# Which flag tile each top-k selection writes: two shared tiles, or tiles by selection

## The chip, the cores and the metric

The kernel runs on one core of a Trainium2 chip. The metric is the time of one execution in microseconds (us) on the device. The engines are named as in the profile: PE (TensorE, matrix products), DVE (VectorE), ACT (ScalarE), POOL (GpSimd) and SP (SyncE, which issues DMAs). Each engine works through its own list of instructions in order.

## The reference

It is one inference step of a two-layer decoder for 1024 prompt tokens and 32 sampled tokens (8 sequences of 4). Layer 0 mixes tokens by a gated MLP. Layer 1 is a sparse attention: an indexer scores every earlier token, the 256 best are kept for each query, and only these are attended to.

```python
def dsa_prompt(h, w_in, w_out):
    q, k, v, qi, ki, wi = dsa_project(h, w_in, pos)
    k_top = min(TOPK_MAX, T // 4)                      # 256
    ...
        sc = index_scores(qi_b, wi_b, ki)
        sc = jnp.where(pos[None, None, :] <= tq[None, :, None], sc, -jnp.inf)
        _, idx = lax.top_k(sc, k_top)
        valid = idx <= tq[None, :, None]
        return attend(q_b, k[bi, idx], v[bi, idx], valid)
```

The sampled tokens do the same against a paged cache of 1024 older tokens. After the mixer of each layer comes an MLP of width 4096 with a squared relu, and a norm ends the whole.

## The kernel before

The two layers follow each other. This study is about the attention of layer 1, roughly from 1100 to 1720 us of the profiled execution. It has these parts, in the order of the code: the index scores (lines 847 to 903), the projection of the queries (lines 932 to 937, one addition of a DVE step at line 914 per result), keys (`key_tile`, KT at line 207/1010) and values, the attention of the samples against the gathered cache (`sample_keys`, `sample_softmax`, `fetch_values`, `sample_values`), and the attention of the prompt: `scores(j, kv)` for query block j (128 queries) and `values(j, kv)`.

The kernel does not gather the 256 best keys. It finds, for each query, the 256th largest index score, and turns the score row into a bias (0 for a kept key, a huge negative number for a dropped one) that `scores` adds at line 1116. Blocks 0 and 1 have at most 256 keys and need no selection. Blocks 2 to 7 have their index scores in SC[2] to SC[7] (128 x 384 up to 128 x 1024); in lists of the order these tiles carry the numbers 11964 to 11969. The samples' scores are SCS, a part of the tile ssum.

`topk` does four selections; the text calls them by their tags:

- a: the samples, one row of 1028 keys, rounds on ACT;
- b: blocks 2 and 3, rounds on DVE;
- c: blocks 4 and 5, rounds on ACT;
- d: blocks 6 and 7, rounds on DVE.

A selection first counts how many scores are at least 0 and then fixes the threshold bit by bit, in 31 rounds. A round on DVE is one count per block (line 705: compare, add up, and write the flags, which nobody reads, to a flag tile) and two small steps (lines 719 and 720). A round on ACT is one Sign per block (line 726, which writes a flag tile too) and three small DVE steps (lines 728 to 730); a selection on ACT ends with one more count per block on DVE at line 705. Then lines 737 to 746 turn the scores into the bias ("marking"). The small tiles of a selection are called sma to smd in the profile.

All counts on DVE write `junk_v` and all Signs on ACT write `junk_a`. The order on each engine is not the order of the code: the framework schedules the instructions along a simulated time line, and keeps only the orders that the tiles ask for. Two writes to one tile stay in the order of the code, also where both are on one engine and nobody reads what they wrote.

Of the kernel before, what the change touches and what calls it, by code (L numbers as in the profile page):

```python
# [14 lines left out]
I8 = mybir.dt.int8  # L15
AF = mybir.ActivationFunctionType
# [5 lines left out]
P = 128  # L22
# [17 lines left out]
L_S = PAST + 4  # L40
# [9 lines left out]
def toks(i):  # L50
    return (i * P, min(T, (i + 1) * P))
# [82 lines left out]
def build(nc, tc, I, O):  # L134
    ctx = ExitStack()
    V, S, G, PE, SP = nc.vector, nc.scalar, nc.gpsimd, nc.tensor, nc.sync

    def pool(name, stack=ctx, **k):
        return stack.enter_context(tc.tile_pool(name=name, bufs=k.pop("bufs", 1), **k))
# [14 lines left out]
    def f(ap):  # L154
        return ap.bitcast(F32)
# [196 lines left out]
    for i0, i1 in ((0, 1), (1, 3), (3, 6), (6, 9)):  # L352
# [3 lines left out]
        for k0 in range(0, NK, g):  # L356
            p = ps("px" if k0 // g % 2 else "pt")
            for k in range(k0, k0 + g):
                for i in range(i0, i1):
                    a, b = toks(i)  # L360
                    o = (k - k0) * w + a - t0
                    PE.transpose(p[:, o:o + b - a], natural(i)[:b - a, k * P:(k + 1) * P], eye[:b - a, :b - a])
            x = al.tile([P, 512], F32, name="xc", bufs=6)
# [13 lines left out]
    for qt in range(4):  # L377
# [22 lines left out]
        for i in range(NT):  # L400
            a, b = toks(i)
# [278 lines left out]
    tkp = pool("tkp", st)  # L680

    def t2(shape, d=F32R, tag="t2"):
        return tkp.tile(shape, d, name=tag, bufs=2 if tag == "tk" else 3)

    junks = [tkp.tile([P, L_S], I8, name="junk%d" % z) for z in range(2)]

    def topk(tag, blocks, how, R):
        nb = len(blocks)
        bank = tkp.tile([P, 7 * nb], F32, name="sm" + tag)
        used = [0]  # L690

        def small(name, d=F32):
            used[0] += nb
            return bank[:, used[0] - nb:used[0]].bitcast(d)

        cnt, s, lim = small("cnt"), small("s"), small("lim")
        cand, nxt, kb = small("cand", I32), small("nxt", I32), small("kb", I32)
        junk_v, junk_a = junks
        eq = small("eq")
        for z in (cnt, eq):  # L700
            G.memset(z, 0.0)

        def count(sc):
            for i, x in enumerate(blocks):
                V.tensor_scalar(junk_v[R, :x.shape[1]], x, sc if isinstance(sc, float) else sc[R, i:i + 1], None,  # L705
                                op0=ALU.is_ge, op1=ALU.add, accum_out=cnt[R, i:i + 1])

        if how == "act":
            for i, x in enumerate(blocks):
                G.memset(lim[:, i:i + 1], x.shape[1] - 2 * TOPK + 0.5)  # L710
        count(0.0)
        V.tensor_scalar(s, cnt, TOPK - 0.5, 2.0, op0=ALU.is_ge, op1=ALU.mult)
        V.tensor_scalar(s, s, 1.0, None, op0=ALU.subtract)
        V.tensor_scalar(cand, cnt, TOPK - 0.5, -1.0, op0=ALU.is_lt, op1=ALU.mult)
        V.tensor_scalar(cand, cand, 1 << 30, None, op0=ALU.bitwise_xor)
        if how == "vec":
            for bit in range(30, -1, -1):
                count(f(cand))
                V.tensor_scalar(kb, cnt, TOPK - 0.5, float(1 << bit), op0=ALU.is_lt, op1=ALU.mult)
                V.scalar_tensor_tensor(cand, kb, 1 << (bit - 1) if bit else 0, cand, op0=ALU.bitwise_xor,  # L720
                                       op1=ALU.bitwise_xor)
        else:
            for bit in range(30, -1, -1):
                for i, x in enumerate(blocks):
                    L = x.shape[1]
                    S.activation(junk_a[R, :L], x, AF.Sign, bias=f(cand)[R, i:i + 1], scale=-1.0,
                                 accum_out=cnt[R, i:i + 1])
                V.tensor_scalar(nxt, cand, 1 << (bit - 1) if bit else 0, None, op0=ALU.bitwise_xor)  # L728
                V.tensor_tensor(kb, cnt, lim, op=ALU.is_gt)
                V.scalar_tensor_tensor(cand, kb, bit, nxt, op0=ALU.logical_shift_left, op1=ALU.bitwise_xor)  # L730
            V.tensor_copy(kb, s)
            V.tensor_tensor(nxt, cand, kb, op=ALU.add)
            count(f(nxt))
            V.scalar_tensor_tensor(kb, cnt, TOPK - 0.5, s, op0=ALU.is_ge, op1=ALU.mult)
            V.tensor_tensor(cand, cand, kb, op=ALU.add)
        need = lim
        V.tensor_scalar(s, f(cand), -1.0, None, op0=ALU.mult)
        for i, x in enumerate(blocks):
            sg, e = (t2([P, L_S], d, "tk")[R, :x.shape[1]] for d in (BF16, F16))
            S.activation(sg, x, AF.Sign, bias=s[R, i:i + 1], accum_out=cnt[R, i:i + 1])  # L740
            V.tensor_scalar(e, sg, 0.0, None, op0=ALU.is_equal, op1=ALU.add, accum_out=eq[R, i:i + 1])
            V.tensor_tensor(need[:, i:i + 1], eq[:, i:i + 1], cnt[:, i:i + 1], op=ALU.subtract)
            V.tensor_scalar(need[:, i:i + 1], need[:, i:i + 1], 0.5, TOPK + 0.25 - x.shape[1] / 2, op0=ALU.mult, op1=ALU.add)
            V.tensor_tensor_scan(e, e, e, 0.0, ALU.add, ALU.max)
            V.scalar_tensor_tensor(x, e, need[R, i:i + 1], sg, op0=ALU.is_gt, op1=ALU.is_le)
            G.tensor_scalar(x, x, -DROP, DROP, op0=ALU.mult, op1=ALU.add)
# [16 lines left out]
    def select(where):  # L763
        for z, (blks, how, w) in enumerate(TOPK_GROUPS):
            if w == where:
                topk("abcdef"[z], [SCS if j == "S" else SC[j] for j in blks], how, SB if "S" in blks else slice(0, P))
# [80 lines left out]
    for i in (8, 0, 1, 2, 3, 4, 5, 6, 7):  # L847
        a, b = toks(i)
# [384 lines left out]
def trace(inputs):  # L1233
    import concourse.bacc as bacc

    nc = bacc.Bacc("TRN2", target_bir_lowering=False, num_devices=1)
    arrays, I, O = {}, {}, {}
    data = {n: np.ascontiguousarray(inputs[n]) for n in INS}
    data["one"], data["one_a"], data["ropeq"] = ONE, ONE_A, ROPEQ
    for n, a in data.items():  # L1240
        arrays["in_" + n] = a
        I[n] = nc.dram_tensor("in_" + n, a.shape, mybir.dt.from_np(a.dtype), kind="ExternalInput").ap()
    for n, s in OUTS:
        O[n] = nc.dram_tensor("out_" + n, s, F32, kind="ExternalOutput").ap()
    with tile.TileContext(nc, schedule_with_timeline_sim=True) as tc:
        build(nc, tc, I, O)
    return nc, arrays
# [8 lines left out]
```

## Time and profile before

| | us |
|---|---|
| median of 3 runs (2542.66 to 2546.99) | 2546.78 |
| the profiled execution | 2550.52 |
| its span, first to last instruction | 2548.4 |

Against the span, PE is busy for 92%, DVE for 67%, POOL for 51%, ACT for 42%. The granted TensorE clock is 0.969 of full speed in the mean. The shares are means over a long kernel, in most of which PE never stops; what counts for this change is the stretch from 1138 to 1720 us.

### The profile page before, as it was taken

How to read it: one execution, taken by the hardware profiler on the slowest of the kernel's cores; microseconds unless marked ns; L12 is line 12 of the kernel's file. 1: busy time of each engine (PE TensorE's matmuls, PEld its weight loads, DVE VectorE, ACT ScalarE, POOL GpSimd, SP SyncE). 2: the span in 40 equal slices, each digit the busy share in tenths (PEclk: the TensorE clock that was granted, in tenths of full speed). 3: DMA queues.
4: the chain of work that ended last, by engine and by line, in shares of the span. 5: the costliest groups of instructions: out<-in, count | busy, mean ns of one | idle time of the engine just before them, and what ended most of it. 6: DMA issues, size and time to landing. Idle time of an engine off the chain costs nothing.

```text
span 2548.4 us, 42829 instructions
## 1 busy us (share of the span) xinstructions
PE 2356.4 (92%) x16001; PEld 2250.2 (88%) x16001; DVE 1712.3 (67%) x3730; ACT 1063.9 (42%) x2161; POOL 1310.0 (51%) x1695
## 2 busy tenths in 40 slices
PE   8999999999999999999888786199999999999998
PEld 8999999999999999878876565089999999999998
DVE  6241277777777777836873289963777777777775
ACT  5223243333333333548426874152433333333335
POOL 2246347667666676422333342032466566666764
PEclk9999999999999999999989798599999999999999
DMA  6111301111111111322233510004111111111111
GB/s 230 50 44 50 110 30 46 51 42 51 46 47 50 47 46 51 107 61 78 67 95 116 192 26 9 0 22 143 32 46 53 42 44 53 47 50 42 51 51 69
DMA packets 180800, 158.46 MB, mean 62 GB/s; under 512 B 10376, under 2 KB 169712, under 8 KB 179568
## 3 DMA queue, kind: packets, MB, share of 16 engines
q1 hardware_dynamic: 176496, 136.86, 17.4%
q0 software_dynamic: 4096, 18.88, 2.2%
q8 instruction: 125, 2.05, 0.3%
q14 instruction: 83, 0.68, 0.1%
HBM read 134.24 MB, written 21.47 MB: 61 GB/s over the span
## 4 chain that ended last, share of the span: by engine, by line
PE 31%; DVE 10%; POOL 5%; issue 5%; DMA 3%; ACT 3%; SPq 0%; DVEq 0%; POOLq 0%; ACTq 0%
PE ps L245 4%; PE ps L250 3%; PE ps L251 3%; DVE junk L705 3%; PE px L245 3%; PE px L251 3%; PE px L250 3%; PE ps L593 1%; PE ps L594 1%; PE ps L595 1%; POOL st L561 1%; DMA qd<-scr 1%; DMA raw<-in_cache_k,idh 1%; PE pt L595 1%; PE pt L594 1%
## 5 line engine op out<-in xcount | busy, mean ns | idle before, releaser
L584 POOL TENSOR_TENSOR X<-X,scr 128x264 f32<-128x264 f32 x480 | 427.7, 915 | 166.3 <-DVE X L584 119.5
L245 PE MATMUL ps<-h,w 128*128 128x384 f32 (+1 forms) x1344 | 436.9, 325 | 3.5 <-DVE sma L728 3.0
L251 PE MATMUL ps<-h,w 128*128 128x384 f32 (+1 forms) x1344 | 434.2, 323 | 1.6 <-POOL w L207 1.4
L250 PE MATMUL ps<-h,w 128*128 128x384 f32 (+1 forms) x1344 | 434.7, 323 | 0.0
L206 ACT ACTIVATE w<-raw 128x1024 fp32r<-128x1024 f32 (+2 forms) x248 | 250.8, 1013 | 315.2 <-PE px L250 122.8
L207 DVE TENSOR_TENSOR w<-raw,w 128x1024 fp32r<-128x1024 f32 (+1 forms) x211 | 296.6, 1406 | 36.5 <-ACT w L206 36.1
L245 PE MATMUL px<-h,w 128*128 128x384 f32 (+1 forms) x960 | 311.9, 325 | 0.3
L250 PE MATMUL px<-h,w 128*128 128x384 f32 (+1 forms) x960 | 309.3, 322 | 0.0
L251 PE MATMUL px<-h,w 128*128 128x384 f32 (+1 forms) x960 | 308.7, 322 | 0.0
L606 ACT ACTIVATE scr<-ps 128x264 f32<-128x264 f32 x240 | 92.7, 386 | 425.5 <-PE ps L595 375.7
L245 PEld LDWEIGHTS ps<-h,w 128*128 128x128 f32 x1344 | 253.4, 189 | 5.2 <-DVE sma L728 3.3
L251 PEld LDWEIGHTS ps<-h,w 128*128 128x128 f32 x1344 | 253.3, 188 | 3.1 <-POOL w L207 1.7
L250 PEld LDWEIGHTS ps<-h,w 128*128 128x128 f32 x1344 | 253.3, 188 | 0.7
L584 DVE TENSOR_TENSOR X<-X,ps 128x264 f32<-128x264 f32 x480 | 197.5, 422 | 63.6 <-PE ps L595 63.6
L584 DVE TENSOR_TENSOR X<-X,px 128x264 f32<-128x264 f32 x480 | 194.4, 422 | 53.4 <-PE px L595 53.4
L593 PE MATMUL ps<-A,w 128*128 128x264 f32 x720 | 206.9, 288 | 20.8 <-ACT A L206 20.8
L584 DVE TENSOR_TENSOR X<-X,pt 128x264 f32<-128x264 f32 x480 | 203.3, 424 | 33.8 <-PE pt L595 28.8
L594 PE MATMUL ps<-A,w 128*128 128x264 f32 x720 | 206.4, 290 | 7.2 <-DVE A L207 7.0
L595 PE MATMUL ps<-A,w 128*128 128x264 f32 x720 | 203.4, 284 | 0.0
L571 POOL TENSOR_TENSOR raw<-raw 128x128 f32<-128x128 f32 x120 | 56.9, 474 | 268.9 <-DMA raw<-in_ffn_w 178.6
L207 DVE TENSOR_TENSOR A<-st,A 128x264 fp32r<-128x264 f32 (+2 forms) x184 | 163.8, 902 | 45.9 <-ACT A L206 45.9
L245 PEld LDWEIGHTS px<-h,w 128*128 128x128 f32 x960 | 180.3, 188 | 1.8 <-DVE X L584 1.7
(396 smaller groups left out, 6353.5 us busy)
## 6 DMA issues: line engine op xcount, KB each, us to landing
raw<-in_ffn_w SPq DMA_DIRECT2D x68, 512.0 KB
raw<-in_ffn_w SPq DMA_DIRECT2D x120, 256.0 KB
X<-xd SPq DMA_DIRECT2D x16, 528.0 KB
raw<-in_a_w_in SPq DMA_DIRECT2D x10, 512.0 KB
GV<-in_x_prompt SPq DMA_DIRECT2D x8, 512.0 KB
raw<-in_a_w_out SPq DMA_DIRECT2D x8, 512.0 KB
raw<-in_b_w_in SPq DMA_DIRECT2D x8, 512.0 KB
raw<-in_b_w_out SPq DMA_DIRECT2D x8, 512.0 KB
```

The lines of the kernel that those rows point to most:

```text
L206: S.activation(hi, src, AF.Copy)
L207: (lo_w[0] or V).tensor_tensor(lo, src, f(hi), op=ALU.subtract)
L245: PE.matmul(out, lh, rh, start=first, stop=False)
L250: PE.matmul(out, lh, rl, start=False, stop=False)
L251: PE.matmul(out, ll, rh, start=False, stop=last)
L571: G.tensor_tensor(sm[0], a21, a22, op=ALU.add)
L584: eng.tensor_tensor(x, x, src, op=op)
L593: PE.matmul(p, wh, xh, start=first, stop=False, skip_group_check=not first)
L594: PE.matmul(p, wh, xl, start=False, stop=False, skip_group_check=not first)
L595: PE.matmul(p, wl, xh, start=False, stop=True, skip_group_check=not first)
L606: S.activation(u, p, AF.Copy)
L705: V.tensor_scalar(junk_v[R, :x.shape[1]], x, sc if isinstance(sc, float) else sc[R, i:i + 1], None, op0=ALU.is_ge, op1=ALU.add, accum_out= ...
```

## The change

The two shared flag tiles go. Selections a, b and c each get a flag tile of their own, used by both their engines; selection d writes the tile of a (the tag is the letter; the condition is true for d alone).

```diff
-    junks = [tkp.tile([P, L_S], I8, name="junk%d" % z) for z in range(2)]
+    junks = {}
...
-        junk_v, junk_a = junks
+        if how == "vec" and tag != "b":
+            junk = junks["a"]
+        else:
+            junk = junks[tag] = tkp.tile([P, max(x.shape[1] for x in blocks)], I8, name="junk" + tag)
...
-                V.tensor_scalar(junk_v[R, :x.shape[1]], x, sc if isinstance(sc, float) else sc[R, i:i + 1], None,
+                V.tensor_scalar(junk[R, :x.shape[1]], x, sc if isinstance(sc, float) else sc[R, i:i + 1], None,
                                 op0=ALU.is_ge, op1=ALU.add, accum_out=cnt[R, i:i + 1])
...
-                    S.activation(junk_a[R, :L], x, AF.Sign, bias=f(cand)[R, i:i + 1], scale=-1.0,
+                    S.activation(junk[R, :L], x, AF.Sign, bias=f(cand)[R, i:i + 1], scale=-1.0,
                                  accum_out=cnt[R, i:i + 1])
```

No instruction is added or removed: each engine has as many as before. The tiles take 1028, 512 and 768 bytes of each partition where they took twice 1028. What changes is the order that the scheduler makes. In the changed kernel's lists the line numbers behind line 697 are higher by 3 (705 is 708).

First place, DVE: the first count of b. Before it stands here, behind the last count of a (the third row is a's last count, the last row b's first, on SC[2]):

```order
L900 SCALAR_TENSOR_TENSOR sc_11967<-r,wsc,sc_11967 128x384
L732 ISA sma<-sma 128x2
L705 TENSOR_SCALAR junk_11973,sma<-ssum,sma 32x1028
L900 SCALAR_TENSOR_TENSOR sc_11967<-r,wsc,sc_11967 128x384
L914 TENSOR_TENSOR scr<-ps,rbc 128x384
L734 SCALAR_TENSOR_TENSOR sma<-sma 128x1
L705 TENSOR_SCALAR junk_11973,smb<-sc_11964 128x384
```

Now, on DVE, in the middle of the index scores of block 4 (tile 11966), rounds of b (smb) and rounds of a (sma) stand in turns:

```order
L708 TENSOR_SCALAR junkb,smb<-sc_11964,smb 128x384
L732 TENSOR_TENSOR sma<-sma 128x1
L708 TENSOR_SCALAR junkb,smb<-sc_11965,smb 128x512
L733 SCALAR_TENSOR_TENSOR sma<-sma 128x1
L917 TENSOR_TENSOR scr<-ps,rbc 128x384
L903 SCALAR_TENSOR_TENSOR sc_11966<-r,wsc,sc_11966 128x320
L722 TENSOR_SCALAR smb<-smb 128x2
L731 TENSOR_SCALAR sma<-sma 128x1
L903 SCALAR_TENSOR_TENSOR sc_11966<-r,wsc,sc_11966 128x320
L723 SCALAR_TENSOR_TENSOR smb<-smb 128x2
```

So b has moved from behind all of a, where block 5 was being scored, to its scores' own readiness.

Second place, DVE: the end of the rounds of d, and the first step of the prompt's attention that stands behind it. Before, it is the first step of `scores(6)` (L1116 on tile 11968, block 6):

```order
L705 TENSOR_SCALAR junk_11973,smd<-sc_11969,smd 128x1024
L719 TENSOR_SCALAR smd<-smd 128x2
L720 SCALAR_TENSOR_TENSOR smd<-smd 128x2
L737 TENSOR_SCALAR smd<-smd 128x2
L741 TENSOR_SCALAR tk,smd<-tk 128x896
L742 TENSOR_TENSOR smd<-smd 128x1
L744 SCALAR_TENSOR_TENSOR tk<-tk 128x896
L743 TENSOR_SCALAR smd<-smd 128x1
L745 SCALAR_TENSOR_TENSOR sc_11968<-tk,smd 128x896
L1116 ISA w,mx<-px,sc_11968 128x448
```

Now, on DVE, the rounds of d end inside the second `sample_softmax` (L1044), and what stands behind them is the first step of `scores(0)` (L1119 on the causal mask, in the tile one):

```order
L1044 ISA mxs 128x1
L723 SCALAR_TENSOR_TENSOR smd<-smd 128x2
L1044 ISA w,mxs<-ps,w,mxs 128x260
L1044 ISA mxs 128x1
L740 TENSOR_SCALAR smd<-smd 128x2
L955 RECIPROCAL rc<-sd 128x1
L744 TENSOR_SCALAR tk,smd<-tk 128x896
L1056 TENSOR_TENSOR pn<-w,one 128x32
L745 TENSOR_TENSOR smd<-smd 128x1
L747 SCALAR_TENSOR_TENSOR tk<-tk 128x896
L746 TENSOR_SCALAR smd<-smd 128x1
L1119 ISA w,mx<-px,one 128x128
```

The whole of d has moved ahead of the whole of the prompt's attention. Third place, DVE, right behind the last index score of block 7: where before only rounds of b stood, rounds of d, c and b now share the engine:

```order
L708 TENSOR_SCALAR junka,smd<-sc_11968,smd 128x896
L731 TENSOR_SCALAR smc<-smc 128x2
L708 TENSOR_SCALAR junkb,smb<-sc_11964,smb 128x384
L917 TENSOR_TENSOR scr<-ps,rbc 128x384
L708 TENSOR_SCALAR junka,smd<-sc_11969,smd 128x1024
L708 TENSOR_SCALAR junkb,smb<-sc_11965,smb 128x512
L732 TENSOR_TENSOR smc<-smc 128x2
L722 TENSOR_SCALAR smd<-smd 128x2
L722 TENSOR_SCALAR smb<-smb 128x2
L733 SCALAR_TENSOR_TENSOR smc<-smc 128x2
```

Counted over the whole order of DVE, so many rounds of the 31 stand ahead of three steps that both kernels have:

| rounds ahead of | before: a, b, c, d | now: a, b, c, d |
|---|---|---|
| the mask of block 7 (L902), the end of the index scores | 31, 11, 0, 0 | 31, 25, 10, 0 |
| the index copy of `fetch_values` (L1064) | 31, 31, 11, 0 | 31, 31, 30, 22 |
| the first step of `scores(0)` (L1116) | 31, 31, 23, 0 | 31, 31, 31, 31 |

## Rows read from the trace of the kernel before

**Rows 1.** The page: busy tenths of PE, granted TensorE clock, 40 slices.

```profile
PE   8999999999999999999888786199999999999998
PEclk9999999999999999999989798599999999999999
```

**Rows 2.** Windows: start:end, length, busy us by engine, PEclk, DMA share, GB/s.

```profile
1138.00:1293.00 155.00, 141.75 (x847) 134.51 (x846) 119.81 (x314) 102.73 (x186) 39.63 (x38) 0.98 0.22 65
1293.00:1415.00 122.00, 101.43 (x699) 83.76 (x698) 55.80 (x195) 61.69 (x141) 48.47 (x92) 0.89 0.37 115
1415.00:1455.00 40.00, 25.15 (x146) 18.15 (x145) 8.73 (x41) 31.96 (x70) 13.76 (x15) 0.77 0.65 243
1455.00:1577.00 122.00, 105.52 (x643) 78.22 (x641) 108.46 (x345) 85.85 (x209) 47.22 (x62) 0.95 0.11 28
1577.00:1647.00 70.00, 0.00 (x0) 0.00 (x1) 64.62 (x141) 2.64 (x5) 0.94 (x1) 0.52 0.00 0
1647.00:1720.00 73.00, 70.07 (x355) 56.35 (x356) 48.29 (x118) 39.41 (x69) 22.78 (x20) 0.95 0.06 18
```

**Rows 3.** Waits of PE, 1475 to 1720: us in total, times, longest.

```profile
PE px L245 <- DVE mx L1116: 75.1, 4, 70.4
```

**Rows 4.** Timeline of PE: start, us, operation, [idle before <- releaser].

```profile
1647.00 0.74 PE L245 MATMUL px<-KT,t 128*128 128x448 f32 x1 [70.37 <-DVE mx L1116]
```

**Rows 5.** Timeline of DVE: score blocks ready (L902), counts (L705).

```profile
1173.27 0.29 DVE L902 TENSOR_TENSOR sc<-sc,one 128x128 f32<-128x128 f32 x1
...
1225.57 1.27 DVE L705 TENSOR_SCALAR_CACHE_REDUCE junk<-ssum,sma 32x1028 int8<-32x1028 f32 x1
...
1227.95 0.55 DVE L705 TENSOR_SCALAR_CACHE_REDUCE junk<-sc 128x384 int8<-128x384 f32 x1
...
1230.72 0.28 DVE L902 TENSOR_TENSOR sc<-sc,one 128x128 f32<-128x128 f32 x1
...
1292.47 0.28 DVE L902 TENSOR_TENSOR sc<-sc,one 128x128 f32<-128x128 f32 x1
...
1349.61 0.81 DVE L705 TENSOR_SCALAR_CACHE_REDUCE junk<-sc 128x640 int8<-128x640 f32 x1
...
1501.02 1.07 DVE L705 TENSOR_SCALAR_CACHE_REDUCE junk<-sc 128x896 int8<-128x896 f32 x1
```

**Rows 6.** Timeline of DVE: starts of two rounds of b, two of d.

```profile
1299.89 0.60 DVE L705 TENSOR_SCALAR_CACHE_REDUCE junk<-sc,smb 128x384 int8<-128x384 f32 x1
...
1301.73 0.61 DVE L705 TENSOR_SCALAR_CACHE_REDUCE junk<-sc,smb 128x384 int8<-128x384 f32 x1
...
1578.30 1.15 DVE L705 TENSOR_SCALAR_CACHE_REDUCE junk<-sc,smd 128x896 int8<-128x896 f32 x1
...
1581.21 1.15 DVE L705 TENSOR_SCALAR_CACHE_REDUCE junk<-sc,smd 128x896 int8<-128x896 f32 x1
```

**Rows 7.** Groups by shape, DVE, 1138 to 1650: busy, mean ns | idle before, releasers.

```profile
L914 DVE TENSOR_TENSOR scr<-ps,rbc 128x384 f32<-128x384 f32 x16 | 8.9, 555 | 10.2 <-DMA qd<-scr 3.7 <-POOL scr L928 3.6 <-PE ps L251 2.9
L729 DVE TENSOR_TENSOR smc<-smc 128x2 int32<-128x2 f32 x31 | 7.5, 243 | 53.2 <-ACT junk L726 53.2
L728 DVE TENSOR_SCALAR smc<-smc 128x2 int32<-128x2 int32 x31 | 6.4, 206 | 1.0
L729 DVE TENSOR_TENSOR sma<-sma 128x1 int32<-128x1 f32 x31 | 6.1, 196 | 15.3 <-ACT junk L726 15.1
L730 DVE SCALAR_TENSOR_TENSOR smc<-smc 128x2 int32<-128x2 int32 x31 | 5.6, 180 | 1.0
L207 DVE TENSOR_TENSOR KT<-pt,KT 128x256 fp32r<-128x256 f32 x8 | 3.4, 422 | 10.3 <-ACT KT L206 10.3
```

**Rows 8.** One line's instructions (L719): ns min/median/max, first and last start.

```profile
L719 DVE TENSOR_SCALAR smb<-smb x31: 154/169/1387, 1237.4 to 1349.5; 128x2 int32<-128x2 f32 x31
L719 DVE TENSOR_SCALAR smd<-smd x31: 149/169/509, 1513.2 to 1639.0; 128x2 int32<-128x2 f32 x31
```

**Rows 9.** The Signs of c on ACT, by tile.

```profile
L726 ACT ACTIVATE junk<-sc,smc x62: 812/888/978, 1354.0 to 1496.3; 128x640 int8<-128x640 f32 x31, 128x768 int8<-128x768 f32 x31
```

## The prediction

> **What bounds the kernel now.** I begin with the page's slices: PE is at nine tenths nearly everywhere, except around the slices from 1300 us on, with a hole of two slices in which the clock falls too [rows 1]. So I cut the attention of layer 1 into six stretches with the windows [rows 2]. In the stretch from 1577 to 1647 PE does nothing at all, while DVE is busy for 64.6 of 70 us. The waits of PE say for what: 75.1 us in four waits for DVE's step at L1116, one of 70.4 us [rows 3]; the timeline shows that one ending at 1647.00 with the first product of `scores(6)` in a new bank [rows 4]. L1116 adds the bias of block 6, and that is made by selection d, whose rounds run until 1639 [rows 8].
>
> Why is d so late? The timeline of DVE has each block's readiness and each selection's first count [rows 5]. SC[3] is ready at 1173.5, b starts at 1227.95, right behind the last count of a (1225.57). SC[5] is ready at 1231.0, c starts at 1349.6, when b's rounds are over. SC[7] is ready at 1292.8, d starts its first count at 1501.0, when c's are. The scores are ready 54, 118 and 208 us before they are used. No data goes from one selection to the next; what they share is the flag tile of the counts. The four therefore run one behind the other, and the last leaves DVE as the only working engine.
>
> **What the change removes.** With tiles of their own, b and c may start when their scores are there; d shares only with a, which ends early. The order shows that this happens: ahead of the first step of `scores(0)` stand all 31 rounds of d, where none stood. So the wait of 70.4 us [rows 4] has nothing left to wait for. I take 70, the length of the stretch, and count the restart in the last term.
>
> **What it costs.** The same rounds now stand on DVE ahead of the prompt's attention, and an engine works in order: the steps of index scores, queries, keys and `scores(0)` queue behind them. I sum DVE's work in the three stretches before 1455, where `scores(0)` starts, from its busy time [rows 2] and the rounds that the order moves. A round of b costs 1301.73 - 1299.89 = 1.84 us, one of d 1581.21 - 1578.30 = 2.91 [rows 6], the three small steps of a round of c 0.243 + 0.206 + 0.180 = 0.63 [rows 7].
> First stretch (to the end of the index scores): 119.8, plus 14 rounds of b 25.8, plus 10 of c 6.3, plus three first counts of c and d (0.8 to 1.1 each, [rows 5]) 2.9: 154.8 us of 155.
> Second (to `fetch_values`): 55.8, less 14 rounds of b 25.8, plus 9 of c 5.7, plus 22 of d 64.0, less c's first counts 1.8, plus one of d 1.2: 99.1 of 122.
> Third (to `scores(0)`): 8.7, less 11 rounds of c 6.9, plus 9 of d 26.2, plus about 9 (my estimate, from the blocks' widths) for the last counts and the marking of c: 37 of 40.
> Together 291 us of work where 317 pass. It fits, if DVE never waits; it does wait. Of its idle time, 10.2 us before L914 and 10.3 before KT come from DMAs, POOL, PE and ACT, which the change does not touch; the 15.3 for a's Signs stay in part, as b's rounds now fill them; the 53.2 for c's Signs [rows 7] shrink, since a count of d of 1.2 us now stands where DVE idled, against about 1.8 us of two Signs [rows 9]. I let 15 us remain in the first stretch, which is full, some 27 in the second, which has 23 of room, and 6 in the third, which has 3. The overrun is 15 + 4 + 3 = 22 us. Bounds: nothing, if the rounds fill every gap; and 107 (35 + 43 + 29, all that is added), if not one of them falls into idle time. I take the low part, since DVE in the stretch from 1455 to 1577, where rounds and other work stand mixed already, is busy for 108.5 of 122 us, 89% [rows 2], and 291 at 89% are 327, ten more than pass.
>
> **VectorE and GpSimd.** The rounds of d move from a stretch in which POOL works 0.94 of 70 us into one with 48.5 of 122 [rows 2]. The small step L719 shows what may come of it: the median is 169 ns for b and for d, the longest is 1387 for b, which ran beside a busy POOL, and 509 for d [rows 8]. If every third round of d's 31 lost 1.2 us so, that would be 12 us; I leave it inside the 22 and the range. The Trainium skill (SBUF — State Buffer, Who interferes with whom) states that VectorE and GpSimd share a port pair as an exclusive lock, taken by VectorE instructions with two SBUF inputs or in a two-port mode, but not by the form of tensor_scalar that writes its accumulator. By that rule only the small steps can be blocked, never the counts, which fits these rows; were all 31 rounds blocked once for the longest excess, the sum would be 37 us worse and the time 2522.
>
> **What else follows.** From 1455 to 1720 the prompt's attention took 265 us, 70 of them the stall. In the other 195 PE is busy for 105.5 + 70.1 = 175.6 and idle for 19.4, at a clock of 0.95 [rows 2]. The rounds of c and d leave this stretch, which frees over 40 us of DVE, and without the stall there is no restart at the lower clock (0.52 in the stall is near the lower of the two levels, 1.2 GHz). Full clock would give back 5% of 175.6, 9 us, and half the idle time another 10. I take 14; bounds 5 and 28. The Signs of c cost ACT the same, earlier: its stretches have 155 - 103 and 122 - 62 us free [rows 2], and c brings 10 rounds into the first. I cost that at nothing; if ACT were late, DVE's small steps of c would wait, which is in the overrun. SP's and POOL's orders change at a few places, for nothing by my count, since their waits end with data.
>
> **The sum** against the profiled execution: 2550.5 - 70 - 14 + 22 = 2488.5. That execution is 3.7 us above the median, so the forecast is 2546.8 - 62 = 2485. A change within 0.2% (5 us) is about what a measurement here can't tell from none.
>
> **Rivals.** (1) The waits of DVE are longer than I say: the chains of a, b, c and d wait for one another in one queue, each small step of c for ACT, with everything behind it. Half of the 107 us unhidden is 53; with 10 from the attention the gain is 27, the time 2520. For it speaks that 53.2 us were idled for c alone [rows 7]; against it, that the third stretch has nothing else to do than these rounds. (2) Slower: the first stretch is full by my sum, and there the index scores feed PE through ACT; if the added rounds hide nowhere, 107 - 70 - 14 gives +23, 2570. It decides from an overrun of 84 us on, almost four times mine. (3) The change does not do what it says, because another wait ends at the same place, the marking on POOL or c's 62 Signs: about 2547. Against it, the order has c and d finished before `scores(0)`, 100 us of PE work ahead of their first use. (4) Better: the gaps take all the rounds and the attention gives 28: 2449.
>
> **How the numbers follow.** My forecast, 2463 to 2514 by the bounds of the overrun (0 to 45), 0.58. Better than that 0.15. A gain of 5 to 33 us, rival 1, 0.16. No change 0.04, slower 0.07. From these faster is 0.89, same 0.04, slower 0.07. The range 2450 to 2525 leaves out the two slow cases, part of rival 1 and the last of rival 4.
>
> **What would show it.** Right: no wait of PE of over 10 us at L1116; rounds of b from about 1180, c from 1240, d from 1310; DVE over 85% busy from 1138 to about 1475; `scores(0)` 10 to 35 us later than 1455; from there to the end of the attention about 180 us. The terms are wrong if the index scores end after 1320 (the first overrun is larger), or if DVE idles for c's Signs as long as before. The prediction fails if PE waits for L1116 as long as before at `scores(0)` instead of `scores(6)`: then the stall has only moved to the front.

## The result and the profile after

The changed kernel takes 2450.26 us (median of 4 runs, 2447.63 to 2453.22), the kernel before in the same series 2546.23. The ratio is 0.9626, 95% interval 0.9609 to 0.9643: 96 us or 3.7% faster. The forecast was 2485, 62 us faster; the result lies 0.3 us inside the lower edge of the range, and the same kernel measured again (e11) took 2447.1 us, outside it. That the first number fell inside is luck. The direction and the mechanism were right, the size was short by 34 us.

The profiled execution has a span of 2451.1 us (before 2548.4). Its page, busy tenths of PE and granted clock in 40 slices, as in [rows 1]:

```profile
PE   8999999999999999989987879999999999999998
PEclk9999999999999999999999879999999999999999
```

The hole of two slices is gone, and with it the dip of the clock. The waits of PE from the start of the prompt's attention (1463.7 us) to its end (us in total, times, longest), which answer to [rows 3]:

```profile
PE ps L245 <- ACT w L206: 1.1, 1, 1.1
PE px L251 <- POOL t L207: 0.4, 1, 0.4
```

No wait for DVE's step that adds the bias (now L1119) is left. Where the rounds went is seen by tile, for b, c and d (start of the first and the last):

```profile
L708 DVE TENSOR_SCALAR_CACHE_REDUCE junkb<-sc,smb x62: 597/672/746, 1179.2 to 1323.7; 128x384 int8<-128x384 f32 x31, 128x512 int8<-128x512 f32 x31
...
L729 ACT ACTIVATE junkc<-sc,smc x62: 811/875/958, 1235.0 to 1418.7; 128x640 int8<-128x640 f32 x31, 128x768 int8<-128x768 f32 x31
...
L708 DVE TENSOR_SCALAR_CACHE_REDUCE junka<-sc,smd x62: 1133/1204/1282, 1300.3 to 1455.0; 128x896 int8<-128x896 f32 x31, 128x1024 int8<-128x1024 f32 x31
```

The rounds of b begin at 1179, where even its first count came at 1228 [rows 5]; the first Sign of c comes 119 us earlier than in [rows 9]; the rounds of d begin at 1300, where its first count came at 1501. The three overlap, and the last small step of d starts at 1457.5, ahead of the attention's start at 1463.7.

To see where the 97.3 us of the span come from, I take four steps of DVE that every kernel here has: the first use of the mask (block 0, the start of the prompt's attention), of c's bias (block 4, 128x320), of d's bias (block 6, 128x448) and the last one. First the timeline of DVE before, then after:

```profile
1455.59 0.28 DVE L1116 CUSTOM_DVE_ANT_0 w<-px,one 128x128 f32<-128x128 f32 x1
...
1513.87 0.47 DVE L1116 CUSTOM_DVE_ANT_0 w<-px,sc 128x320 f32<-128x320 f32 x1
...
1646.31 0.62 DVE L1116 CUSTOM_DVE_ANT_0 w<-px,sc 128x448 f32<-128x448 f32 x1 [1.06 <-POOL sc L746]
...
1691.79 0.74 DVE L1116 CUSTOM_DVE_ANT_0 w<-px,sc,mx 128x512 f32<-128x512 f32 x1
```

```profile
1463.73 0.28 DVE L1119 CUSTOM_DVE_ANT_0 w<-px,one 128x128 f32<-128x128 f32 x1
...
1504.84 0.48 DVE L1119 CUSTOM_DVE_ANT_0 w<-px,sc 128x320 f32<-128x320 f32 x1
...
1549.04 0.61 DVE L1119 CUSTOM_DVE_ANT_0 w<-px,sc 128x448 f32<-128x448 f32 x1
...
1595.16 0.74 DVE L1119 CUSTOM_DVE_ANT_0 w<-px,sc,mx 128x512 f32<-128x512 f32 x1
```

From these I form three intervals: A from block 0 to block 4, B from block 4 to block 6, C from block 6 to the last step. The table has them for the experiments too (us; each worked out from such rows of that kernel's profiled execution). The medians come from several series, in which the kernel before took 2546.2 to 2549.6 us; the ratios compare within a series. The marks are steps of DVE, so an interval does not hold the same PE work in every kernel: PE's products recorded in A, B without the stall, and C are 353, 288 and 198 before, 322, 268 and 254 after. The sum of the three is what can be compared most safely.

| kernel | median | ratio to before | start | A | B | C |
|---|---|---|---|---|---|---|
| before | 2546.2 | 1 | 1455.6 | 58.3 | 132.4 | 45.5 |
| changed | 2450.3 | 0.9626 | 1463.7 | 41.1 | 44.2 | 46.1 |
| changed, again (e11) | 2447.1 | 0.9610 | 1455.4 | 41.3 | 44.2 | 46.1 |
| e1 c writes a's tile, d its own | 2447.4 | 0.9608 | 1456.8 | 43.4 | 44.2 | 46.1 |
| e2 d writes c's tile | 2483.8 | 0.9746 | 1459.6 | 48.1 | 75.7 | 45.3 |
| e3 before, d with 9 rounds | 2485.5 | 0.9751 | 1457.5 | 58.3 | 68.1 | 46.5 |
| e4 only d has its own | 2491.6 | 0.9780 | 1449.4 | 92.1 | 46.1 | 46.0 |
| e5 changed, d with 8 rounds | 2450.7 | 0.9608 | 1461.0 | 42.5 | 44.2 | 46.1 |
| e6 changed, b counts twice | 2465.6 | 0.9677 | 1456.5 | 53.5 | 51.5 | 46.1 |
| e7 only c has its own | 2455.9 | 0.9635 | 1442.8 | 46.4 | 52.2 | 50.7 |
| e8 changed, scores(0) ahead of the softmax | 2456.3 | 0.9637 | 1455.8 | 55.5 | 44.7 | 46.1 |
| e9 before, d with 1 round | 2466.9 | 0.9685 | 1452.4 | 58.5 | 48.7 | 46.0 |
| e10 = e1, again | 2447.2 | 0.9602 | 1457.8 | 42.9 | 44.2 | 46.1 |
| e12 two tiles, a+c and b+d | 2452.5 | 0.9629 | 1458.4 | 46.4 | 44.3 | 46.3 |

In the profiled execution the start is 8.1 us later, A is 17.2 shorter and B 88.2, of which 70.4 are the stall of [rows 4] and 17.8 the rest; C is about the same (0.6 longer). 70.4 + 17.2 + 17.8 - 8.1 = 97.3. The windows of the changed kernel (columns as in [rows 2]) up to the start, up to the first use of d's bias, and the end of the attention:

```profile
1138.00:1463.70 325.70, 274.51 (x1715) 243.25 (x1715) 269.88 (x797) 212.87 (x435) 102.06 (x149) 0.91 0.33 106
1463.70:1549.00 85.30, 84.78 (x588) 68.63 (x578) 68.98 (x234) 65.54 (x164) 48.49 (x62) 0.99 0.13 32
1549.00:1623.00 74.00, 72.89 (x407) 61.42 (x406) 49.62 (x125) 44.66 (x79) 20.91 (x19) 1.00 0.08 23
```

In the attention PE is idle for 0.5 + 1.1 = 1.6 us, where it was idle for 19.4 beside the stall [rows 2], and its 995 products are busy for 157.7 us instead of 175.6. So both halves of the extra gain are there: 18 us of idle time and 18 of PE's busy time. The second is not all shorter products: nine products of the samples' softmax (L1050 and L1056), whose durations make 3.8 us, lie just inside the window before (from 1455) and just ahead of it now.

### The profile page after: what moved, and what is told of

It is laid out like the page before. It is cut to its first block, busy times and chain, and to the rows that moved or that the text cites. A ratio compares the mean times of both kernels' runs of the same rounds, so it can differ in the third digit from the quotient of the medians.

```text
span 2451.1 us, 42867 instructions
## 1 busy us (share of the span) xinstructions
PE 2341.6 (96%) x16001; PEld 2250.3 (92%) x16001; DVE 1689.3 (69%) x3730; ACT 1062.5 (43%) x2161; POOL 1314.2 (54%) x1695
## 4 chain that ended last, share of the span: by engine, by line
PE 36%; DVE 7%; POOL 4%; DMA 3%; issue 3%; ACT 2%; SPq 0%; DVEq 0%; POOLq 0%; ACTq 0%
PE ps L245 4%; PE ps L251 4%; PE ps L250 4%; PE px L245 3%; PE px L251 3%; PE px L250 3%; PE ps L593 2%; PE ps L594 1%; PE ps L595 1%; POOL st L561 1%; DVE sc L903 1%; PE pt L1132 1%; PE pt L595 1%; PE pt L594 1%; PE pt L593 1%
## 5 line engine op out<-in xcount | busy, mean ns | idle before, releaser
L584 POOL TENSOR_TENSOR X<-X,scr 128x264 f32<-128x264 f32 x480 | 434.7, 930 | 168.2 <-DVE X L584 119.6
L207 DVE TENSOR_TENSOR w<-raw,w 128x1024 fp32r<-128x1024 f32 (+1 forms) x211 | 292.4, 1386 | 37.7 <-ACT w L206 37.3
L571 POOL TENSOR_TENSOR raw<-raw 128x128 f32<-128x128 f32 x120 | 55.5, 462 | 262.3 <-DMA raw<-in_ffn_w 172.5
L207 DVE TENSOR_TENSOR A<-st,A 128x264 fp32r<-128x264 f32 (+2 forms) x184 | 163.5, 901 | 44.9 <-ACT A L206 44.8
```

Source lines behind the costliest of these rows:

```text
L207: (lo_w[0] or V).tensor_tensor(lo, src, f(hi), op=ALU.subtract)
L571: G.tensor_tensor(sm[0], a21, a22, op=ALU.add)
L584: eng.tensor_tensor(x, x, src, op=op)
```

## The experiments

Theory A, as the result left it: a shared flag tile costs only where the earlier selection still works when the scores of the later one are ready; the gain is the stall, plus A and B, in which rounds of c and d no longer stand among the steps of the attention; and the rounds that now stand ahead of the attention lie in idle time of DVE. The rivals: the sharing with a matters; the 35 us belong to the stall, as restart and piled-up work; a fixed share of the moved rounds is not hidden.

### Which sharing costs

**e1**, from the changed kernel. c and d swap places in the memory:

```diff
-        if how == "vec" and tag != "b":
+        if tag == "c":
             junk = junks["a"]
```

> The tiles dealt out another way: c writes the tile of a, and d has its own. Theory A (a shared tile costs only where the earlier selection is still at work when the scores of the later one are ready): a ends at 1257 us and c could start at 1231, so c starts some 25 us later than in the changed kernel, still long before its bias is wanted at about 1500: 2450 us, within 5. Rival (any sharing with a puts work into the full stretch before the queries' projection, or d was held by a): 2460 and more for the first, under 2443 for the second.

Measured: 2447.43 us, 0.9608 (0.9592 to 0.9624). The first Sign of c is at 1259 instead of 1235, as expected, and B and C are those of the changed kernel. Since this is at the edge of what a measurement can tell, the two kernels ran once more together:

> The first experiment's kernel beside the changed one on one chip. Theory A (which selection shares with a doesn't matter): a ratio to the kernel before that lies within 0.2% of the changed kernel's. Rival (d held by a's tile, or room in the first stretch since c starts later): 0.2% to 0.4% faster than the changed kernel.

> The changed kernel once more, as a yardstick for the run before it: 0.9626 of the kernel before, within 0.002.

Measured: 0.9602 (0.9589 to 0.9615) for e10 and 0.9610 (0.9596 to 0.9623) for e11, 2447.2 and 2447.1 us. They are the same within the intervals: whether c or d shares with a, which ends at 1257, makes no difference that these runs can tell.

**e2**, from the changed kernel. Now d shares with one that is not done in time (the tile of c is made 1024 wide):

```diff
-        if how == "vec" and tag != "b":
-            junk = junks["a"]
+        if tag == "d":
+            junk = junks["c"]
```

> d writes the tile of c in place of that of a, b has its own. Theory A: d can't start before c's last count at about 1425 us, so 20 of its 31 rounds stand among the steps of the prompt's attention, where DVE has some 16 of 86 us free; the attention is slower by 30 to 55 us than in the changed kernel, without one long stall: 2490 us (2480 to 2505). Rival 1 (only the one long stall counted, and rounds among the attention are hidden): 2455. Rival 2 (d is late again and PE stalls for it as before): 2530.

Measured: 2483.84 us, 0.9746 (0.9730 to 0.9763). The rounds of d, by tile, and then the longest group of PE's waits from 1440 to 1620:

```profile
L708 DVE TENSOR_SCALAR_CACHE_REDUCE junkc<-sc,smd x62: 1129/1201/1280, 1410.3 to 1574.7; 128x896 int8<-128x896 f32 x31, 128x1024 int8<-128x1024 f32 x31
```

```profile
PE px L245 <- DVE mx L1119: 14.2, 5, 10.7
```

So d starts 110 us later than in the changed kernel, though only the tile differs, and 34 of the 96 us are lost again (31 by the ratios). The wait of 10.7 us, which ends with d's bias at 1584, explains a third of it; the rest lies in A (48.1 us instead of 41.1) and in B, 75.7 us long with that wait instead of 44.2, where DVE is busy for 72.8 us. Theory A holds, rival 1 (2455) and rival 2 (2530) fall.

**e4**, from the kernel before: only d leaves the row (one tile is shared by a, b and c on both engines).

```diff
-        junk_v, junk_a = junks
+        junk_v = junk_a = junks[0] if tag != "d" else tkp.tile([P, 1024], I8, name="junk" + tag)
```

> One tile for a, b and c, and one for d: only d leaves the row of selections, and c is behind b as before and now beside d. Theory A: d's stall of 70 us goes, but 21 of c's rounds stand behind the start of the prompt's attention (in the kernel before 8), so the attention waits for c's bias at block 4 instead: about 2505 us (2485 to 2525). Rival (the long stall was all that cost): 2450 to 2476.

Measured: 2491.57 us, 0.9780 (0.9762 to 0.9797); theory A gave 2505 (2485 to 2525). B falls to 46.1, but A grows to 92.1, and the timeline of PE names the place:

```profile
1542.02 0.63 PE L245 MATMUL px<-KT,t 128*128 128x320 f32 x1 [27.08 <-DVE mx L1116]
```

That wait ends with the first step on c's bias (block 4, 320 columns, at 1541). The stall has moved from d to c. To free the last in the row is not enough.

**e7**, the same with c in place of d (`tag != "c"`):

> One tile for a, b and d, and one for c: only c leaves the row, d follows b directly. By the order 18 of d's rounds stand ahead of the attention and 13 among it, all of c ahead of it. Theory A: c's bias is early, so block 4 doesn't wait, d ends some 40 us behind its place in the changed kernel and its 13 rounds slow the first blocks by what DVE has not idle: 2470 us (2460 to 2482), the time from the start of the attention to the first use of d's bias 100 to 112 us (85 in the changed kernel, 124 with d behind c). Rival (a stall for d remains, as in the kernel before): 2500 and more.

Measured: 2455.9 us, 0.9635 (0.9620 to 0.9649). This was a miss, and neither theory had it: A and B together are 98.6 us, a little under what was expected (100 to 112), but the attention starts at 1442.8, 13 us earlier than in the kernel before. Ahead of the start PE did as much as in the others (window to that point, columns as in [rows 2]):

```profile
1138.00:1442.80 304.80, 268.10 (x1694) 235.12 (x1696) 243.05 (x708) 212.29 (x435) 108.30 (x146) 0.94 0.35 113
```

PE is idle there for 36.7 us, in the changed kernel for 51.2. One of the waits that shrink is PE's longest wait for the gather of the samples' keys, 2.3 us here, 9.2 in the changed kernel. That is half of the 14.5 us. Why this order of the rounds suits that stretch is not settled: each of these edits moves the order of every engine, not only that of the rounds. The early start is given back in the attention, where 13 rounds of d stand: A, B and C are 17.9 us longer than in the changed kernel.

**e12**, from the changed kernel: as many tiles as before, two of 1028 bytes, but dealt out by selection instead of by engine.

```diff
-        if how == "vec" and tag != "b":
-            junk = junks["a"]
+        if tag in "cd":
+            junk = junks["ab"["cd".index(tag)]]
```

> Two tiles of 1028 bytes, as many as in the kernel before, but dealt out by selection and not by engine: a and c share one, b and d the other. By the order 20 rounds of d stand ahead of the value fetch and all 31 ahead of the prompt's attention, as in the changed kernel. Theory A (it counts only whether the earlier sharer is done in time, not how many tiles there are): a is done some 25 us, b some 30 us after c's and d's scores are ready, which the attention doesn't notice: 0.960 to 0.963 of the kernel before, about 2450 us. Rival (the later start of d pushes its end into the attention, as where d followed b and c was free): 0.964 to 0.970.

Measured: 2452.54 us, 0.9629 (0.9616 to 0.9642). The ratio is that of the first measurement of the changed kernel and 0.2% above the second, so all but a few us of the gain are there, with no byte more than before. The rounds of d, by tile:

```profile
L708 DVE TENSOR_SCALAR_CACHE_REDUCE junkb<-sc,smd x62: 1131/1208/1281, 1313.5 to 1453.5; 128x896 int8<-128x896 f32 x31, 128x1024 int8<-128x1024 f32 x31
```

d waits for b here, and starts 13 us later than in the changed kernel. The attention hardly notices: B and C are the same, A is 5 us longer (46.4), with 1.8 us of waits of PE for L1119 and a granted clock of 0.89 in A, where it was 0.98. Four tiles, one for each selection, were not tried.

### What the 35 us beyond the stall are

**e3** and **e9**, from the kernel before: its order, with fewer rounds of d (9 and 1).

```diff
-            for bit in range(30, -1, -1):
+            for bit in range(30, 21 if tag == "d" else -1, -1):
                 count(f(cand))
```

> The kernel before, with 9 of d's 31 rounds; 22 rounds are left out, so the bias of blocks 6 and 7 is not the reference's. Order and tiles are as before. It takes 22 x 2.91 = 64 us out of the stall and moves nothing else. Theory A (the changed kernel's 35 us beyond the stall came from rounds of c and d that no longer stand among the attention of blocks 0 to 5): they are still there, so only the 64 go: 2483 us (2478 to 2488). Rival (the 35 us belonged to the stall itself, as restart at a low clock and work that piled up behind it): 2450 to 2460.

> The kernel before with one of d's 31 rounds; 30 are left out, so the bias of blocks 6 and 7 is not the reference's. The order of the rest is that of before. With 9 rounds it took 2485.5 us and no long stall was left, only 8 rounds among the steps of blocks 4 and 5. Theory A (rounds among the attention's steps delay PE): the 8 rounds are 23 us of DVE's work in a stretch where DVE is busy for 66 of 69 us, so most of it comes back: 2466 us (2458 to 2472), and the time from the first use of c's bias to the first of d's falls from 68 us to 45 to 52. Rival (the attention of blocks 4 and 5 is held by c's lateness and by PE's own work, the rounds of d beside it are free): 2480 to 2486.

Measured: 2485.54 us, 0.9751 (0.9732 to 0.9769) for e3, and 2466.92, 0.9685 (0.9670 to 0.9700) for e9. With 9 rounds the long stall is gone (PE waits for L1116 for 9.7 us in four pieces), but B is still 68.1 us long and the time 35 us above the changed kernel. With one round B falls by another 19.4, and as A and C stay within 0.6 us, so does the whole attention. That is 2.4 us for each of the 8 rounds (2.1 by the ratios), against 2.91 of DVE's work [rows 6]. PE's waits for the steps on d's bias (448 columns), 6.3 us of the 9.7 in e3, are gone in e9. Another wait that falls is that of PE's values products for the addition of DVE at L207, which stands in the same queue as the rounds, in e3 and then in e9 (us in total, times, longest):

```profile
PE ps L248 <- DVE raw L207: 9.9, 12, 2.0
```

```profile
PE ps L248 <- DVE raw L207: 5.0, 6, 1.4
```

In the kernel before it was 8.1 us in ten waits; in the changed kernel none is left. So of the 17.8 us of B at least 13 are rounds of d among the steps of blocks 4 and 5 (62.0 without the stall, 48.7 in e9), not a consequence of the stall. Half of e9's gain over e3 is PE's idle time, which falls from 26.1 to 15.8 us over A, B and C; the other half is busy time of PE, 146.8 against 137.4 us for 840 and 841 products. A stays at 58.5 us in e9, so its 17.2 have nothing to do with d. What is left there is c: 8 of its rounds by the order, its marking at 1504 to 1522 and its bias that is used at 1513.9. e4, which makes c later still, makes A longer still. Which part of A is the late bias, which the rounds beside the steps, and which the 31 products of PE that the kernel before does in A and the changed one elsewhere, is not separated. PE's idle time in A is 7.5 us before and 0.5 after.

### What the rounds cost ahead of the attention

**e5**, the changed kernel with the same edit, 8 rounds for d (`range(30, 22 ...`):

> The changed kernel with 8 of d's 31 rounds; 23 are left out, so the bias of blocks 6 and 7 is not the reference's. It takes 67 us of DVE's work from the time between the last index score and the start of the prompt's attention (41 before the value fetch, 26 behind it). Theory A (the rounds lie in gaps of DVE, and the 6 to 8 us by which the changed kernel comes later to the start of the attention are all that they cost): 2444 us (2440 to 2449), the attention starting at 1456 to 1460 us. Rival (a fixed share of the rounds is not hidden, 30% as the prediction had it): 2430.

Measured: 2450.71 us, 0.9608 (0.9595 to 0.9622), as the second measurement of the changed kernel (0.9610) and 0.2% below the first (0.9626). The window up to the start:

```profile
1138.00:1461.00 323.00, 272.54 (x1698) 239.34 (x1696) 215.48 (x666) 213.02 (x436) 106.19 (x150) 0.92 0.32 104
```

DVE is busy for 215 us instead of 270, and the stretch is as long. The rival's 2430 falls. Theory A's range (2440 to 2449) is missed by the median, but the kernel before took 2549.6 us in this series; by the ratios the 23 rounds are worth 0 to 5 us, too little to tell apart from nothing. The same shows without any edit in e11, the changed kernel in another execution: with DVE busy for 267.6 us the stretch is 317.4 us long, and 1455.6 - 1138 = 317.6 before. The 8.1 us of the first profile are no more than one execution differs from another; a price of the change is not shown.

**e6**, the changed kernel with more load:

```diff
             for bit in range(30, -1, -1):
-                count(f(cand))
+                for again in range(2 if tag == "b" else 1):
+                    count(f(cand))
```

> The changed kernel with every count of b made twice: 57 us more of DVE's work, which the order puts mostly behind the last index score; 5 rounds of d go behind the start of the attention. Theory A (free as long as the stretch has idle time on DVE, full price beyond): the second stretch has 33 us of room and takes its part, the third has 4.6 of room and gets 17 more, the attention gets 15 more where it has 16: 2468 us (2460 to 2480). Rival 1 (all hidden): 2450 to 2454. Rival 2 (DVE is the bound before the attention already, so all of it shows): 2507.

Measured: 2465.58 us, 0.9677 (0.9662 to 0.9691), 0.5% to 0.7% or 13 to 17 us above the changed kernel in its two measurements; theory A gave 18. But it does not test what I meant it to. The added work is less than the 57 us that I put down: a whole round of b is 1.84 us, its two counts alone are 1301.33 - 1299.89 = 1.44, so 45 us. And DVE is not busier ahead of the start than in the changed kernel (269.9 and 267.6 us):

```profile
1138.00:1456.40 318.40, 269.14 (x1681) 238.41 (x1680) 269.50 (x856) 209.12 (x427) 97.79 (x142) 0.90 0.34 108
```

The order has put about as much work behind the start as was added ahead of it: 5 rounds of d (14.6 us), the end of b's marking (1458 to 1465) and the marking of c (1468 to 1482), which the changed kernel has ahead of it. There A and B are longer by 20. So e6 shows that what is pushed behind the start is paid for; how much room was left ahead of it, it doesn't show.

**e8**, the changed kernel with one statement moved:

```diff
-    sample_softmax(1)
     probs = [scores(0, kv) for kv in range(2)]
+    sample_softmax(1)
```

> The changed kernel with the first scores of the prompt's attention written ahead of the second softmax of the samples: the order then has their steps some ten places earlier on DVE and ACT, and the samples' softmax behind them. Theory A (ahead of the attention PE waits for the samples' gather and DVE has little left to give): the same within 4 us, 2446 to 2452. Rival (PE's 16 idle us there can be filled with the first scores): 2436 to 2442.

Measured: 2456.31 us, 0.9637 (0.9624 to 0.9650), 0.1% to 0.3% above the changed kernel in its two measurements. This was a miss: it is above theory A's range, and the rival fell the other way. The first step of `scores(0)` comes at 1455.8, no earlier than in e11, and A is 55.5 us long, since the samples' softmax now stands in it; PE waits there for 8.5 us in four pieces for a step of POOL at L956, and for 3.8 for L1119. PE's gaps ahead of the attention are not filled by starting the attention earlier in the code.

## Why the prediction was right in kind and short in size

**The stall**, -70: right. It is gone whole, and no other wait for a bias has taken its place, at `scores(0)`, `scores(4)` or `scores(6)`. The cause that the rows gave (four selections in a row by their flag tile, and nothing else between them) is shown by e1, e2 and e12: the same code with the tile of another selection starts d at 1299, 1410 or 1313.

**The overrun ahead of the attention**, +22: mis-sized; it measured 8.1 in one execution and -0.2 in the other, and by e5 the rounds of d have little or no part in it. I had let 15, 27 and 6 us of waits of DVE remain beside a full load. In fact the rounds stood in those waits: DVE's idle time for c's Signs fell from 53.2 us [rows 7] to 5.2, and DVE is busy for 269.9 of 325.7 us up to the start, 83%. My sum of the work up to there, 291 us, was 21 too high, as much as the term itself. The added durations were not too long: summed one by one over the timeline, DVE's instructions up to the start last 204 us before and 321 after, 116 more, and I had added 107. But they overlap more. The time that they cover, which is what the windows call busy, is 184 us before and 270 after. In the stall, where only steps of d follow each other, L719 and L720 start 0.19 us apart (1577.91 and 1578.10, 0.16 long each); now a step of c and one of d start 0.08 apart (1334.22 and 1334.30, 0.16 long each). I priced each round by its time alone on the engine, and among the steps of other selections it takes less.

**What else follows in the attention**, -14 (bounds 5 to 28): mis-sized, the measured 35 lie outside the bounds. I priced what the rounds' departure gives back as half of PE's idle time and 5% of clock, 10 + 9 = 19, and then took 14 without a reason. Nearly all of the idle time went (19.4 to 1.6 us), and PE's busy time fell by 18 us, not 9. A clock of 0.95 explains 9 of these, the nine products at the window's border up to 3.8; what the rest is stays open. The step that failed is the half: I left PE idle time that the rounds caused, since I took DVE's 89% in that stretch (in the term on the overrun) as a proof that rounds and other work mix well. It was the opposite: there PE waited for steps of DVE that stood behind the rounds, and a round cost 2.4 us (e3 against e9). The same round is nearly free in the stretch ahead (e5) and mostly paid there. Block 4's bias came late as well; its share of A is open.

The two misses go one way: in the profiled execution the overrun was 14 us too high and the attention 21 too low, 35 together, which is the sum's 2488.5 against 2453.2. One bound was also summed wrongly: an overrun of 45 instead of 22 gives 2508, not 2514. It changes nothing here.

**The small steps beside GpSimd**, up to 12 us inside the 22: the steps did get longer, by less. Groups by shape in the changed kernel:

```profile
L722 DVE TENSOR_SCALAR smd<-smd 128x2 int32<-128x2 f32 x31 | 7.9, 255 | 0.1
...
L708 DVE TENSOR_SCALAR_CACHE_REDUCE junka<-sc,smd 128x1024 int8<-128x1024 f32 x31 | 39.5, 1275 | 0.5
```

The step of d takes 255 ns in the mean, where before (L719 then) it took 176: 2.4 us over 31 rounds. The median is 161; one step of 2307 ns makes most of the difference, and no row shows what held it. The counts take 1275 ns in the mean, the same as before. By the rule in the Trainium skill (SBUF — State Buffer, Who interferes with whom) the counts can't be held by GpSimd; these rows agree.

**The signs to look for.** b, c and d came at 1179, 1235 and 1300 (said: 1180, 1240, 1310). The start of the attention was 8 us later or not at all (said: 10 to 35), the attention from there about 159 us long (said: 180). DVE is busy for 83% of the stretch up to the start (said: over 85). Of the rivals, the fourth came, "the gaps take all the rounds and the attention gives 28", at 2449; it had 0.15. It put both terms at their ends, and they came out near those or beyond.

## What to carry to other kernels

Under this framework a scratch tile that nobody reads still orders its writers, on one engine and across engines; who shares it with whom decides more than how many there are. Pair those that are not at work at the same time: two tiles dealt out by selection gave here what the two dealt out by engine had cost, 95 us.

When work moves from one stretch to another, price it twice, by what it will cost where it goes and by what it costs where it stands now. DVE, 89% busy beside a PE with 16 us of idle time in 122, was being waited for here; the same work was nearly free where DVE waited for others.

## What the runs showed of the hardware that I had not expected

The restart after the stall, at a granted clock of 0.70 in the 13 us behind it (its window is below), does not show in C: 45.5 us before, 46.1 after. But C holds 198 recorded products before and 254 after, so it was not free. Right behind the stall a product of 448 columns takes 0.57 us, in the changed kernel 0.36 at full clock.

```profile
1647.00:1660.00 13.00, 10.38 (x34) 7.97 (x35) 11.44 (x31) 6.31 (x11) 6.62 (x6) 0.70 0.00 0
```

Two executions of the same changed kernel came to the start of the attention at 1463.7 and 1455.4 us. A difference of 8 us at one point of a single profile was as large as the term that I wanted to read from it.

By the records, instructions of DVE from different selections overlap: up to the start they cover 51 us less than they last (321 and 270), where one selection stood behind the other 20 us less (204 and 184).
